# Rotary halves by transfer, an even filling row in layer 2, 136-column pooling bands and an early Exp table in a two-layer transformer kernel

## The chip, the cores and the metric

The kernel runs on one core of one Trainium2 chip. The time is the device time of one execution in microseconds. The kernel before takes 1686.69 us (median of 3 runs, 1686.47 to 1686.74). Five engines work side by side, each through its own list of instructions in order: PE (matmuls), ACT (activations, casts, copies), DVE (elementwise work and reductions), POOL (a little elementwise work) and SP, which only issues transfers (DMAs). The order on each engine is fixed when the program is built; an instruction waits on semaphores for the engines or transfers that it depends on.

## What is computed

Two transformer layers on 256 tokens of width 1024, with 256 context tokens beside them. A layer is a half feed-forward step, a mixing step and a second half feed-forward step; the last layer updates only the tokens, not the context. In the mixing step one projection gives queries, keys and values for a windowed attention of 4 heads, an input `u` for average pooling over 4 groups of 64 channels, and queries, keys and values for a grouped attention (8 query heads, 2 key heads). The queries and keys of the grouped attention are normalised per head and rotated by position:

```
def _rope_axis(x, ang):
    m = x.shape[-1] // 2
    x1, x2 = x32[..., :m], x32[..., m:]
    return jnp.concatenate([x1 * cos - x2 * sin, x1 * sin + x2 * cos], axis=-1)
...
out = jnp.concatenate([_rope_axis(x[..., :half], ang_row), _rope_axis(x[..., half:], ang_col)], axis=-1)
...
y = (mean - u32.reshape(bn, n, POOL_GROUPS, POOL_GC))     # mean over windows of 2, 4, 8, 16 tokens
y = jnp.einsum('blgc,gcd->blgd', y, w_pool)
```

So within a head of 64 channels, channel i of the first 16 is paired with i + 16, and channel i of the next 16 after 32 with i + 16 again. In between, pieces of the modulation weights `w_ada` for the next phase are multiplied with the two condition vectors.

## The kernel before, in words

Matrices are held feature-major (128 features on the partitions, tokens along the free axis). A float32 product is made of three PE matmuls of split operands (L351, L352, L353, called mm3 below): each weight piece of 1 MB or 0.5 MB is loaded by SP into a `raw` buffer, cast by ACT (L309) and its remainder formed by DVE (L312, "split of a weight"); after the split the `raw` buffer is free and SP may issue the next load into it.

The mixing step in program order: keys and values (`evac_k` writes the grouped keys `kc` with the gain; `k_post` at L915 makes their norms and rotates them), windowed queries, windowed values, and then `run` (L1094), a loop over attention jobs. A job is two heads and 128 tokens: `scores` (L1012, L1013: four matmuls into two PSUM banks), DVE's maximum (L1028 adds the bias of the windowed heads, L1029 reduces), ACT's Exp (L1037), DVE's division by the sum (L1042). Two jobs later `flip` (L1056: eight transposes by PE, L1064: copies by ACT) and, when a pair of heads is whole, `pv` (L1086). Layer 1 has 18 jobs (six of them for the context), layer 2 has 12: four windowed (j0 to j3) and eight grouped ones (j4 to j11).

PE would wait for the softmax between jobs, so other work is put there. `fill(us)` calls `piece()` until a planner's clock has advanced by `us`; `piece()` takes, in this order, the rest of the in-projection (`rest_in`: four chunks c0 to c3 of the grouped queries, 24 matmuls each, then `u`, 24 matmuls for 128 tokens), `pv` of finished windowed heads, `pooled` (L1178), and then by turns a piece of the out-projection and a quantum of the `w_ada` products (L181). How much goes between two jobs is the row `FILL[l]`: entries 2n and 2n+1 stand after the scores of job n and before the flip of job n-2 (for the first two jobs only entry 2n is used, as nothing is flipped yet). The clock has no relation to the chip: matmuls and pooling add fixed numbers to it by `tick`, and `later(us, f)` puts `f` into the program when the clock has moved on by `us`. So a change of a `tick`, of a `FILL` entry or of a `later` moves instructions on all engines.

A finished chunk is evacuated by ACT twice: `qc` with the gain (L1148) and its square (L1150); `qstat` (L1155, weights `hind`) sums the squares per head on PE. After each pair of chunks `q_post` rotates the pair and makes the reciprocal norms on DVE (twelve small instructions, L392 to L1130). Before a grouped job is scored its queries are split by ACT (L892) and DVE (L893). `before(n)` makes the grouped keys at job 2 (ACT L881, DVE L884).

`rotate` (L900): PE multiplies `q` with a 128x128 matrix `rot` of +1 and -1 (L903) that exchanges and signs the halves, DVE multiplies the result with the sine (L906), POOL multiplies `q` with the cosine in place (L907), and DVE adds (L910). It is called once for the keys and twice for the queries in each layer, five matmuls of 256 columns per layer.

`pooled` (L1178) multiplies `u` with band matrices: for each of the 4 groups two matmuls of 128 columns (L1185, bands `pmd`) and two of 8 columns (L1186, L1187, `edge`) for the tokens across the border between the two blocks. It is called twice in layer 1 (tokens, context) and once in layer 2. ACT copies the result `y` (L1190), PE multiplies it with `pwbd` (L1195).

PSUM has 5 banks for products and scores, 2 for transposes and statistics (`aux`), and 1 for the `w_ada` products.

Of the kernel before, what the change touches and what calls it, by code (L numbers as in the profile page):

```python
# [38 lines left out]
FILL = ((3.3, 2.6, 1.8, 2.6, 3.3, 5.5, 0, 0.6, 3.3, 0, 0.6, 1.2, 1.8, 0.6, 4.2, 2.6, 2.6, 0, 0, 0.6, 4.2, 0.6, 1.2, 0, 2.6, 1.2, 0, 1.8, 2.6, 1.2, 2.6, 0, 0.6, 1.2, 0.6, 0.6, 0, 0, 5.5, 2.6), (3.3, 0.6, 2.6, 3.3, 0.6, 3.3, 5.5, 0, 1.8, 1.8, 0.6, 1.8, 0.6, 5.5, 0, 1.2, 1.2, 1.2, 1.2, 1.2, 4.2, 1.2, 0.6, 0.6, 1.8, 0, 2.6, 0.6))  # L39
# [11 lines left out]
def dit_kernel(  # L51
# [790 lines left out]
    def attention(l, a, both):  # L842
# [55 lines left out]
        def rotate(q, n):  # L898

            rp = aux_bank()  # L900
            rv = rp[:, 0:n * TX].rearrange("p (c t) -> p c t", c=n)
            for i in range(n):
                PE.matmul(out=rv[:, i, :], lhsT=rot, rhs=q[:, i, :], start=True, stop=True)  # L903
# [2 lines left out]
            DVE.tensor_tensor(out=tv, in0=rv, in1=rope[:, 1:2, :].to_broadcast([128, n, TX]), op=ALU.mult)  # L906
            POOL.tensor_tensor(out=q, in0=q, in1=rope[:, 0:1, :].to_broadcast([128, n, TX]), op=ALU.mult)  # L907
# [27 lines left out]
        def evac_k(v, pss):  # L935
            lo, hi = v * TX, v * TX + TX
            ACT.activation(out=ksq[:, lo:hi], in_=pss[1][:, 0:TX], func=AF.Square)
            ACT.activation(out=kc[:, lo:hi], in_=pss[1][:, 0:TX], func=AF.Copy, scale=kng(l))
            ACT.copy(out=vcT[:, lo:hi], in_=pss[1][:, TX:NT])

            def split():
                for hp in range(2):
# [180 lines left out]
        def q_post(j):  # L1123

            rotate(qc[:, 2 * j:2 * j + 2, 0:TX], 2)

            def norm():
                o = slice(j * nb * 4, (j + 1) * nb * 4)
                rq = rsqrt(qst[0][:, o], nb * 4, 1.0 / 64)
                DVE.tensor_scalar(out=rq8[:, o], in0=rq, scalar1=0.125, scalar2=None, op0=ALU.mult)  # L1130
                turned[j] = True
            later(2.0, norm)

        def rest_in():

            qst.append(mm_bank())
            for j in range(2):
# [39 lines left out]
        def pooled(v):  # L1177
            ps = mm_bank()  # L1178
            pv_ = ps.rearrange("p (c t) -> p c t", c=2)
            for g in range(4):  # L1180
# [3 lines left out]
                for tb in range(2):  # L1184
                    PE.matmul(out=o[:, tb * 128:(tb + 1) * 128], lhsT=ug[tb], rhs=pmd[tb][:, g * 128:(g + 1) * 128], start=(g < 2 and tb == 0), stop=False)  # L1185
# [362 lines left out]

def _constants():

    ident = np.eye(128, dtype=np.float32)
    rot = np.zeros((128, 128), np.float32)
    for f in range(128):
        i = f % 32
        if i < 16:
            rot[f + 16, f] = -1.0
        else:
            rot[f - 16, f] = 1.0
# [47 lines left out]
```

## Time and profile before

| | |
|---|---|
| median of 3 runs | 1686.69 us (1686.47 to 1686.74) |
| profiled execution | 1686.64 us |
| its span, first to last instruction | 1684.9 us |
| mean granted PE clock | 0.998 |
| busy share PE, DVE, ACT, POOL | 99%, 63%, 39%, 3% |
| instructions | 23252 |
| transfers | 246.97 MB, 147 GB/s |
| attention of layer 1, of layer 2 | about 453 to 560 us, 1389 to 1472 us |

Times in the views are microseconds from the start of the span. A row of the timeline has start, duration, engine, line, operation, written tile and read tiles, and in square brackets the idle time before it and what ended that. Several like instructions in a row are merged ("x8"); one program matmul of float32 operands that are not split appears as two records. A row of the waits has the waiting engine and line, the releasing engine, tile and line, the total, the count and the longest.

### The profile page before, as it was taken

Reading aid. Unit: us, or ns where it says so; the run is one execution under the profiler, and the core shown is the slowest. Engines: PE = TensorE matmul, PEld = TensorE weight load, DVE = VectorE, ACT = ScalarE, POOL = GpSimd, SP = SyncE. Lnnn points to the kernel's source line nnn. Section 1 sums busy time; section 2 is a strip of 40 time slices with the busy share of each in tenths; the row PEclk is TensorE's granted clock in tenths of the full one; section 3 lists DMA queues with packets and bytes.
Section 4 is the critical chain, followed back from the end, with each engine's and each line's share of the span. In section 5 each row is a group of like instructions: output and inputs, shape, how many; then the busy total and the mean of one; then the engine's idle time right before and its main releaser. Section 6 shows DMA issues by size and latency. Waiting matters only on the chain. (4 is left out here: it accounts for less than half of the span.)

```text
span 1684.9 us, 23252 instructions
## 1 busy us (share of the span) xinstructions
PE 1660.0 (99%) x9256; PEld 1401.6 (83%) x9256; DVE 1055.3 (63%) x1850; ACT 663.8 (39%) x1119; POOL 47.8 (3%) x67
## 2 busy tenths in 40 slices
PE   8999999999999999999999999999999999999997
PEld 5788888889896798888888898888888897799996
DVE  5676567667666776666764476545533567785665
ACT  4332323324556643223233243213232255664543
POOL 0000200000010000000000000020000000010000
PEclk9999999999999999999999999999999999999999
DMA  9755546531305425554553325564533223566551
GB/s 332 206 190 171 161 153 194 167 120 58 113 26 176 132 67 173 166 163 138 175 156 120 87 79 178 161 170 159 155 112 95 81 76 137 202 195 193 179 174 74
DMA packets 284932, 246.97 MB, mean 147 GB/s; under 512 B 9345, under 2 KB 249098, under 8 KB 282776
## 3 DMA queue, kind: packets, MB, share of 16 engines
q1 hardware_dynamic: 281992, 241.30, 46.2%
q0 software_dynamic: 1088, 2.15, 0.6%
q10 hardware_dynamic: 1744, 2.04, 0.4%
q8 instruction: 73, 1.20, 0.3%
q14 instruction: 35, 0.29, 0.1%
HBM read 244.40 MB, written 2.00 MB: 146 GB/s over the span
## 5 line engine op out<-in xcount | busy, mean ns | idle before, releaser
L351 PE MATMUL mm<-act,w 128*128 128x512 f32 (+1 forms) x2016 | 739.1, 367 | 0.0
L352 PE MATMUL mm<-act,w 128*128 128x512 f32 (+1 forms) x2016 | 733.0, 364 | 0.3 <-DVE act L435 0.3
L353 PE MATMUL mm<-act,w 128*128 128x512 f32 (+1 forms) x2016 | 732.9, 364 | 0.0
L312 DVE TENSOR_TENSOR w<-raw,w 128x1024 fp32r<-128x1024 f32 (+1 forms) x307 | 367.6, 1206 | 222.3 <-ACT w L309 221.9
L351 PEld LDWEIGHTS mm<-act,w 128*128 128x128 f32 x2016 | 380.5, 189 | 75.2 <-issue 14.1
L353 PEld LDWEIGHTS mm<-act,w 128*128 128x128 f32 x2016 | 380.4, 189 | 59.7
L352 PEld LDWEIGHTS mm<-act,w 128*128 128x128 f32 x2016 | 380.7, 189 | 59.1 <-DVE act L435 0.5
L309 ACT CAST w<-raw 128x1024 fp32r<-128x1024 f32 (+1 forms) x308 | 313.3, 1031 | 118.8 <-PE mm L353 96.9
L224 DVE SCALAR_TENSOR_TENSOR ada_acc<-ada_raw,sc,ada_acc 128x512 f32<-128x512 f32 x308 | 215.9, 747 | 37.9 <-DMA ada_raw<-in_w_ada_dram 20.9
L562 ACT CAST act<-gf 128x512 fp32r<-128x512 f32 x66 | 40.9, 620 | 269.9 <-DVE gf L559 269.9
L556 ACT ACTIVATE sil<-mm 128x512 f32<-128x512 f32 x66 | 39.3, 596 | 189.4 <-PE mm L353 184.5
L465 DVE SCALAR_TENSOR_TENSOR hT<-mm,hgt,hT 128x256 f32<-128x256 f32 x144 | 63.5, 480 | 76.9 <-PE mm L353 76.6
L559 DVE TENSOR_TENSOR gf<-sil,mm 128x512 f32<-128x512 f32 x65 | 44.7, 687 | 89.5 <-PE mm L353 75.7
L644 PE MATMUL mm<-act,w 128*128 128x258 f32 x352 | 100.2, 285 | 0.0
L645 PE MATMUL mm<-act,w 128*128 128x258 f32 x352 | 99.6, 283 | 0.0
L646 PE MATMUL mm<-act,w 128*128 128x258 f32 x352 | 99.5, 283 | 0.0
L563 DVE TENSOR_TENSOR act<-gf,act 128x512 fp32r<-128x512 f32 x66 | 45.7, 693 | 45.3 <-ACT act L562 45.3
L645 PEld LDWEIGHTS mm<-act,w 128*128 128x128 f32 x352 | 66.8, 190 | 0.3 <-DVE act L618 0.2
L644 PEld LDWEIGHTS mm<-act,w 128*128 128x128 f32 x352 | 66.6, 189 | 0.1
L646 PEld LDWEIGHTS mm<-act,w 128*128 128x128 f32 x352 | 66.4, 189 | 0.0
L377 ACT ACTIVATE sq<-hT 128x256 f32<-128x256 f32 (+1 forms) x45 | 22.5, 500 | 90.8 <-DVE hT L465 90.8
L441 ACT ACTIVATE act<-nt,modT 128x256 fp32r<-128x256 f32 x80 | 39.8, 508 | 37.8 <-DVE nt L440 37.8
(198 smaller groups left out, 1412.1 us busy)
## 6 DMA issues: line engine op xcount, KB each, us to landing
raw<-in_ffn_up_dram SPq DMA_DIRECT2D x170, 512.0 KB
ada_raw<-in_w_ada_dram SPq DMA_DIRECT2D x192, 256.0 KB
raw<-in_ffn_down_dram SPq DMA_DIRECT2D x35, 1024.0 KB
raw<-in_w_ada_dram SPq DMA_DIRECT2D x16, 1024.0 KB
raw<-in_w_in_dram SPq DMA_DIRECT2D x10, 1024.0 KB
raw<-in_ffn_down_dram SPq DMA_DIRECT2D x12, 768.0 KB
raw<-in_w_out_dram SPq DMA_DIRECT2D x8, 1024.0 KB
raw<-in_w_ada_dram SPq DMA_DIRECT2D x12, 512.0 KB
```

The source lines that it names most:

```text
L224: DVE.scalar_tensor_tensor(out=o, in0=raw, scalar=col, in1=o, op0=ALU.mult, op1=ALU.add)
L309: ACT.copy(out=wh, in_=sl)
L312: eng.tensor_tensor(out=wl, in0=sl, in1=wh.bitcast(F32), op=ALU.subtract)
L351: PE.matmul(out=ps, lhsT=wh, rhs=ah, start=start and i == 0, stop=False)
L352: PE.matmul(out=ps, lhsT=wh, rhs=al, start=False, stop=False)
L353: PE.matmul(out=ps, lhsT=wl, rhs=ah, start=False, stop=stop and i == last)
L465: DVE.scalar_tensor_tensor(out=hT[:, k, cols], in0=ps, scalar=gate[:, k, v:v + 1], in1=hT[:, k, cols], op0=ALU.mult, op1=ALU.add)
L559: DVE.tensor_tensor(out=u[:, 0:n], in0=s[:, 0:n], in1=pb[:, 0:n], op=ALU.mult)
L563: DVE.tensor_tensor(out=gl, in0=uv, in1=gh.bitcast(F32), op=ALU.subtract)
L644: PE.matmul(out=ps[:, 0:NX], lhsT=wh, rhs=ah, start=k == 0, stop=False)
L645: PE.matmul(out=ps[:, 0:NX], lhsT=wh, rhs=al, start=False, stop=False)
L646: PE.matmul(out=ps[:, 0:NX], lhsT=wl, rhs=ah, start=False, stop=k == KD - 1)
```

## The change

1. **Rotation.** The matrix `rot` and its matmuls are gone. `swapped` copies the four blocks of 32 partitions crosswise with four SP transfers into `ks` or `qs`: for the keys right after `kc` of the tokens is written, for the queries after each pair of chunks is evacuated. For this the 64 channels of a head are permuted on the host (`HEAD_ORDER`, in the columns of `w_in` for grouped queries and keys and in their gains), so that partners lie 32 partitions apart; the signs go into the sine table. DVE multiplies the swapped tile with the sine in place, both operands now in SBUF, and adds; POOL's cosine product is as before, but writes `q` in place after the transfers have read it. `q_post` is put 5.5 after its pair of chunks by the clock, before 3.0. The tiles `bands`, `qs` and `ks` lie in a part of the layer's activation tile that was unused.
2. **Layer 2's row of FILL**: 28 entries of 1.7 (sum 47.6) in place of 28 different ones (sum 48.9). Layer 1's row is the same.
3. **Pooling**: two matmuls of 136 columns for each group, the second one accumulating on the columns 120 to 256; `tick` 1.1 in place of 1.7.
4. **Exp table**: before the first scores of a layer ACT runs a dummy Exp on one column, so that the table is loaded there.

```diff
-FILL = ((3.3, 2.6, ...), (3.3, 0.6, 2.6, 3.3, 0.6, 3.3, 5.5, 0, 1.8, 1.8, 0.6, 1.8, 0.6, 5.5, 0, 1.2, 1.2, 1.2, 1.2, 1.2, 4.2, 1.2, 0.6, 0.6, 1.8, 0, 2.6, 0.6))
+FILL = ((3.3, 2.6, ...), (1.7,) * 28)
...
+        bands = carve(1088, "p (b g t) -> p b g t", b=2, g=4)
+        qs = carve(1024, "p (c t) -> p c t", c=4)
+        ks = carve(256, "p (c t) -> p c t", c=1)
...
-        def rotate(q, n):
-            rp = aux_bank()
-            rv = rp[:, 0:n * TX].rearrange("p (c t) -> p c t", c=n)
-            for i in range(n):
-                PE.matmul(out=rv[:, i, :], lhsT=rot, rhs=q[:, i, :], start=True, stop=True)
-            t = tmp.tile([128, 512], F32, tag="t2k", bufs=T2K, name="rot_t")
-            tv = t[:, 0:n * TX].rearrange("p (c t) -> p c t", c=n)
-            DVE.tensor_tensor(out=tv, in0=rv, in1=rope[:, 1:2, :].to_broadcast([128, n, TX]), op=ALU.mult)
+        def swapped(dst, src):
+            for p0 in range(0, 128, 32):
+                SP.dma_start(out=dst[p0 ^ 32:(p0 ^ 32) + 32], in_=src[p0:p0 + 32])
+        def rotate(q, other, n):
             POOL.tensor_tensor(out=q, in0=q, in1=rope[:, 0:1, :].to_broadcast([128, n, TX]), op=ALU.mult)
-            def add():
-                DVE.tensor_tensor(out=q, in0=q, in1=tv, op=ALU.add)
-            later(1.5, add)
+            DVE.tensor_tensor(out=other, in0=other, in1=rope[:, 1:2, :].to_broadcast([128, n, TX]), op=ALU.mult)
+            later(1.5, lambda: DVE.tensor_tensor(out=q, in0=q, in1=other, op=ALU.add))
...
             if v:
                 later(0.1, split)
             else:
+                swapped(ks[:, 0], kc[:, 0:TX])
                 split()
...
-            ACT.dma_start(out=pmd[b].rearrange("p (g t) -> p g t", g=4), in_=k_pool[b])
+            ACT.dma_start(out=bands[:, b], in_=k_pool[b])
...
+            if not PT and not sums:
+                warm = small.tile([128, 8], F32, tag="nm", bufs=6, name="nm")
+                ACT.activation(out=warm[:, 0:1], in_=ones, func=AF.Exp)
...
-                later(3.0, lambda j=j: q_post(j))
+                swapped(qs[:, 2 * j:2 * j + 2], qc[:, 2 * j:2 * j + 2, 0:TX])
+                later(5.5, lambda j=j: q_post(j))
...
-                for tb in range(2):
-                    PE.matmul(out=o[:, tb * 128:(tb + 1) * 128], lhsT=ug[tb], rhs=pmd[tb][:, g * 128:(g + 1) * 128], start=(g < 2 and tb == 0), stop=False)
-                PE.matmul(out=o[:, 128:136], lhsT=ug[0], rhs=edge[:, 0, g, :], start=False, stop=False)
-                PE.matmul(out=o[:, 120:128], lhsT=ug[1], rhs=edge[:, 1, g, :], start=False, stop=(g >= 2))
-            tick(1.7)
+                PE.matmul(out=o[:, 0:136], lhsT=ug[0], rhs=bands[:, 0, g], start=g < 2, stop=False, skip_group_check=True)
+                PE.matmul(out=o[:, 120:256], lhsT=ug[1], rhs=bands[:, 1, g], start=False, stop=g >= 2, skip_group_check=True)
+            tick(1.1)
```

In the rows of order below, a line number is that of the kernel which the rows are from: in the kernel after, most lines stand one or two lines earlier (Exp is L1036 there, the chunk's evacuation L1147 and L1149, the transposes L1055). On ACT at the start of layer 2's attention, before, Exp of job j0 (two heads), the evacuation of chunk c0 (`qkv` and `qsq`), Exp of j1, then c1, then the four casts of the grouped keys (`K`), then Exp of j2:

```order
L982 DMA pmd<-in_k_pool_dram 128x512 x2
L1037 ACT_TABLE_LOAD
L1037 ACTIVATE P,sums<-mm,nm 128x512 x2
L1148 ACTIVATE qkv<-mm,colsB 128x256
L1150 ACTIVATE qsq<-mm 128x256
L1037 ACTIVATE P,sums<-mm,nm 128x512 x2
L1148 ACTIVATE qkv<-mm,colsB 128x256
L1150 ACTIVATE qsq<-mm 128x256
L881 CAST K<-qkv 64x512 x4
L1037 ACTIVATE P,sums<-mm,nm 128x512 x2
```

Now, on the same engine at the same place, the table is loaded first, and the Exp of both j0 and j1 stand before the first chunk:

```order
L977 DMA qkv<-in_k_pool_dram 128x544 x2
L1005 ACT_TABLE_LOAD
L1005 ACTIVATE nm<-ones 128x1
L1036 ACTIVATE P,sums<-mm,nm 128x512 x4
L1147 ACTIVATE qkv<-mm,colsB 128x256
L1149 ACTIVATE qsq<-mm 128x256
L880 CAST K<-qkv 64x512 x4
L1036 ACTIVATE P,sums<-mm,nm 128x512 x2
L1147 ACTIVATE qkv<-mm,colsB 128x256
```

The evacuation of c0 moved behind the Exp of j1, and that of c1 behind the casts of the keys and the Exp of j2. On PE the number of in-projection matmuls between the scores of j0 and j1 goes from 36 to 18, between j1 and j2 from 30 to 18.

On PE at the end of layer 2's attention, before (the out-projection's matmuls that lie between are left out at the marks): the scores of the last job j11, a `w_ada` quantum, the transposes of j9, a quantum, those of j10 and of j11, the transposes of the modulation (`adasb`), and the last `pv`:

```order
L1012 MATMUL mm<-K,qst 128x512
L1013 MATMUL mm<-K,qst 128x512
...
L181 MATMUL ada<-raw,sc 32x512 x4
L1056 MATMUL aux<-ident,P 128x128 x8
...
L181 MATMUL ada<-raw,sc 32x512 x4
...
L1056 MATMUL aux<-ident,P 128x128 x8
...
L1056 MATMUL aux<-ident,P 128x128 x8
L249 MATMUL aux<-ident,adasb 128x128 x4
L1086 MATMUL mm<-PT,qkv 64x256 x16
```

Now, on PE at the same place, from the transposes of the modulation on (only the second half of j11's scores is left out):

```order
L247 MATMUL aux<-ident,adasb 128x128 x4
L1055 MATMUL aux<-ident,P 128x128 x4
L1085 MATMUL mm<-PT,qkv 64x256 x16
L1055 MATMUL aux<-ident,P 128x128 x4
L1011 MATMUL mm<-K,qst 128x512
L1012 MATMUL mm<-K,qst 128x512
...
L1055 MATMUL aux<-ident,P 128x128 x24
L1085 MATMUL mm<-PT,qkv 64x256 x16
```

All other pieces stand before the last scores, and 24 transposes in a row follow them. On SP in layer 2, before, the loads of the in-projection, the first out-projection piece and the `w_ada` pieces:

```order
L152 DMA raw<-in_w_in_dram 128x8x256 x4
L150 DMA raw<-in_w_in_dram 128x8x128 x4
L152 DMA raw<-in_w_in_dram 128x8x256
L152 DMA raw<-in_w_out_dram 128x4x512
L157 DMA raw<-in_w_ada_dram 128x2048 x4
```

Now, on SP at the same place, with the swaps of the keys (`32x256`) and of the two query pairs (`32x2x256`) among them:

```order
L150 DMA raw<-in_w_in_dram 128x8x256 x4
L148 DMA raw<-in_w_in_dram 128x8x128 x2
L900 DMA qkv<-qkv 32x256 x4
L148 DMA raw<-in_w_in_dram 128x8x128 x2
L150 DMA raw<-in_w_in_dram 128x8x256
L150 DMA raw<-in_w_out_dram 128x4x512
L155 DMA raw<-in_w_ada_dram 128x2048
L900 DMA qkv<-qkv 32x2x256 x4
L155 DMA raw<-in_w_ada_dram 128x2048
L900 DMA qkv<-qkv 32x2x256 x4
L155 DMA raw<-in_w_ada_dram 128x2048 x2
```

The first query swap stands behind one load of `w_ada`, the second behind two; before, the four loads of `w_ada` followed each other. The other loads keep their order.

More of the change, by code (lines that the diff above doesn't have):

```diff
@@ L38 @@
 DEPTH = (2, 2)
[L39 removed]
+FILL = ((3.3, 2.6, 1.8, 2.6, 3.3, 5.5, 0, 0.6, 3.3, 0, 0.6, 1.2, 1.8, 0.6, 4.2, 2.6, 2.6, 0, 0, 0.6, 4.2, 0.6, 1.2, 0, 2.6, 1.2, 0, 1.8, 2.6, 1.2, 2.6, 0, 0.6, 1.2, 0.6, 0.6, 0, 0, 5.5, 2.6), (1.7,) * 28)
 PACE = (0.8, 0.8, 0.8, 0.8, 0.7, 0.8)
@@ L56, in dit_kernel @@
     na_rpb, pool_w, pool_scale, q_norm_g, k_norm_g, final_g,
-    k_ident, k_rot, k_rope, k_mask, k_pool, k_edge,
+    k_ident, k_rope, k_mask, k_pool,
     out,
@@ L807, in attn_prep @@
             ACT.dma_start(out=mask, in_=k_mask)
-            ACT.dma_start(out=rot, in_=k_rot)
-            ACT.dma_start(out=edge, in_=k_edge)
             ACT.dma_start(out=rope, in_=k_rope.rearrange("s p t -> p s t"))
@@ L977, in attention @@
             pass
-        pmd = [tmp.tile([128, 512], F32, tag="t2k", bufs=T2K, name="pmd") for _ in range(2)]
         for b in range(2):
-            ACT.dma_start(out=pmd[b].rearrange("p (g t) -> p g t", g=4), in_=k_pool[b])
+            ACT.dma_start(out=bands[:, b], in_=k_pool[b])
         rq8 = small.tile([128, 40], F32, tag="rq8", bufs=1, name="rq8")
@@ L1546, in dit_kernel, with _laid_out @@
         flush()
+HEAD_ORDER = np.r_[0:16, 32:48, 16:32, 48:64]
+def _laid_out(name, a):
+    a = np.array(a)
+    if name == "w_in":
+        cols = a[:, :, 1024:1664]
+        a[:, :, 1024:1664] = cols.reshape(a.shape[0], a.shape[1], 10, 64)[..., HEAD_ORDER].reshape(cols.shape)
+    elif name in ("q_norm_g", "k_norm_g"):
+        a = a[:, HEAD_ORDER]
+    return a
 def _constants():
     ident = np.eye(128, dtype=np.float32)
[L1552 to L1558, printed above, removed]
     pos = np.arange(256)
@@ L1563, in _constants @@
     head = np.concatenate([ar, ar, ac, ac], axis=1)
-    ang = np.concatenate([head, head], axis=1).T
-    rope = np.stack([np.cos(ang), np.sin(ang)]).astype(np.float32)
+    ang = np.concatenate([head[:, HEAD_ORDER]] * 2, axis=1).T
+    sign = np.where(np.arange(128) % 64 < 32, -1.0, 1.0)[:, None]
+    rope = np.stack([np.cos(ang), np.sin(ang) * sign]).astype(np.float32)
     col = np.arange(128) % 64
@@ L1575, in _constants @@
             pool[t, g, t] -= np.float32(1.0)
-    blocks = np.stack([pool[0:128, :, 0:128], pool[128:256, :, 128:256]])
-    edge = np.stack([pool[0:128, :, 128:136], pool[128:256, :, 120:128]], axis=1)
-    return {"k_ident": ident, "k_rot": rot, "k_rope": rope, "k_mask": mask, "k_pool": np.ascontiguousarray(blocks), "k_edge": np.ascontiguousarray(edge)}
+    bands = np.stack([pool[0:128, :, 0:136], pool[128:256, :, 120:256]])
+    return {"k_ident": ident, "k_rope": rope, "k_mask": mask, "k_pool": np.ascontiguousarray(bands)}
 _INS = ['x', 'c', 'ctx', 'c_ctx', 'w_ada', 'b_ada', 'norm_g', 'ffn1_up', 'ffn1_down', 'ffn2_up', 'ffn2_down',
         'w_in', 'w_out', 'na_rpb', 'pool_w', 'pool_scale', 'q_norm_g', 'k_norm_g', 'final_g']
-_CONST = ['k_ident', 'k_rot', 'k_rope', 'k_mask', 'k_pool', 'k_edge']
+_CONST = ['k_ident', 'k_rope', 'k_mask', 'k_pool']
 _OUTS = [((1, 256, 1024), 'float32')]
@@ L1594 @@
     for name in _INS + _CONST:
-        a = np.ascontiguousarray(inputs[name] if name in inputs else consts[name])
+        a = np.ascontiguousarray(_laid_out(name, inputs[name]) if name in inputs else consts[name])
         arrays[f"in_{name}_dram"] = a
```

6 lines of the change are left out of this document (2 added, 4 removed).

## The prediction

> **What bounds the kernel now.** I read the page's shares first, then the list of what PE waits for, then stretches of 10 and 20 us around the two attention phases, and last the timelines of the places that the change touches. The page's row of shares:
>
> ```profile
> PE 1660.0 (99%) x9256; PEld 1401.6 (83%) x9256; DVE 1055.3 (63%) x1850; ACT 663.8 (39%) x1119; POOL 47.8 (3%) x67
> ```
>
> PE is busy for 1660.0 of 1684.9 us of span; the others have room. So a gain must take PE work away or close one of PE's few gaps, and a loss must open gaps. PE's waits over the whole program (waiting line, releaser, total, count, longest):
>
> ```profile
> PE aux L927 <- DVE rs_y L401: 2.0, 2, 1.3
> PE mm L1012 <- ACT P L1037: 1.3, 1, 1.3
> PE aux L1056 <- ACT PT L1064: 1.1, 1, 1.1
> PE ada L181 <- DMA raw<-in_w_ada_dram: 1.0, 1, 1.0
> ...
> PE mm L1155 <- DVE rs_v L392: 0.4, 1, 0.4
> ...
> PE aux L249 <- ACT PT L1064: 0.2, 1, 0.2
> PE mm L1185 <- issue: 0.2, 1, 0.2
> ```
>
> Apart from L927, all of these lie in layer 2's attention and sum to 4.2. A stretch of layer 1's attention and two of layer 2's (window, length, busy PE, PEld, DVE, ACT, POOL, clock, DMA share, GB/s):
>
> ```profile
> 500.00:520.00 20.00, 20.00 (x184) 15.53 (x185) 12.35 (x33) 13.80 (x32) 0.00 (x0) 1.00 0.21 62
> ...
> 1400.00:1410.00 10.00, 9.62 (x74) 9.16 (x73) 8.10 (x25) 6.08 (x13) 1.30 (x1) 1.00 0.01 2
> 1410.00:1420.00 10.00, 9.83 (x89) 9.24 (x88) 8.97 (x27) 6.04 (x13) 1.30 (x1) 1.00 0.32 107
> ```
>
> Layer 1 has PE full while DVE and ACT have 6 to 8 of 20 us free: PE work taken away there is time won. In layer 2 DVE is busy for 8 to 9 of 10 us and PE has gaps already: there the order decides.
>
> **Rotation, on PE.** The pair of query matmuls before, the next two products, the three elementwise groups, and the keys' wait (timeline and groups):
>
> ```profile
> 1411.08 1.11 PE L903 MATMUL aux<-qkv,rot 128*128 128x256 f32 x4
> 1411.84 0.47 PE L351 MATMUL mm<-w,act 128*128 128x256 f32 x1
> 1412.15 0.28 PE L352 MATMUL mm<-w,act 128*128 128x256 f32 x1
> 1412.27 0.29 PE L353 MATMUL mm<-w,act 128*128 128x256 f32 x1
> ...
> L906 DVE TENSOR_TENSOR rot_t<-aux,rope x6: 417/688/693, 439.5 to 1412.2; 128x512 f32<-128x512 f32 x4, 128x256 f32<-128x256 f32 x2
> ...
> L907 POOL TENSOR_TENSOR qkv<-qkv,rope x6: 1297/1302/1808, 431.1 to 1412.3; 128x512 f32<-128x512 f32 x4, 128x256 f32<-128x256 f32 x2
> ...
> 1380.83 0.88 PE L927 MATMUL aux<-ident,rs_y 128*64 128x128 f32 x12 [0.76 <-DVE rs_y L401]
> ```
>
> From L903's start to L351's are 0.76, and the first product after it starts 0.19 later than the 0.12 from L352 to L353; part of that stays after any switch. I take 0.8 for a query pair, 1.6 a layer. The keys' matmuls save nothing: L927 waits for DVE's norms, which do not depend on them, so that wait grows by what is saved. DVE's two products per rotation stay at 0.69 each if two SBUF operands cost what one of PSUM did, and POOL's stays at 1.30.
>
> **The swaps.** No transfer between SBUF tiles is in the trace. The nearest row is POOL's 64 KB transfer:
>
> ```profile
> braw<-tab POOLq DMA_DIRECT2D x32, 64.0 KB, 2.4
> ```
>
> A query swap has four of that size; with some 0.3 each for SP's issues it lands about 1.3 + 2.4 = 3.7 after its chunk. The keys' swap has ten us and more before it is used: hidden. The first query swap of layer 1 lands about as late as L906 starts now, with POOL's 1.30 behind it, so the sum on DVE comes up to 1 us later; PE has no gap near it, so it costs 0 to 1, and I take 0.5. The second ones stand on SP behind a `w_ada` load, but DVE wants them some 8 us later.
>
> **Pooling.** The 16 matmuls of a call before, first and following instruction:
>
> ```profile
> 508.40 0.60 PE L1185 MATMUL mm<-pmd,qkv 128*64 128x128 f32 x4
> ...
> 510.60 0.66 PE L1061 MATMUL aux<-ident,P 128*128 128x128 f32 x4
> ```
>
> 2.2 from one start to the other, or 2.0 without the 0.2 of a switch. The columns stay the same, 128 + 128 + 8 + 8 or 136 + 136 a group; the matmuls are halved. So the gain lies between 0 (columns alone) and 1.0 a call (number alone). I take the price per column of the rotation's matmuls, 0.76 for 512 columns: 0.20 for 136, 1.6 a call, 0.4 saved; 0.8 in layer 1 and 0.4 in layer 2. Layer 1 then gives -1.6 - 0.8 + 0.5 = -1.9. The loads of the bands keep their place on ACT's queue.
>
> **Layer 2: the row of FILL and the table.** ACT, DVE and PE at its start, before:
>
> ```profile
> 1388.82 0.40 PE L1012 MATMUL mm<-K,qst 128*128 128x512 f32 x1
> 1396.00 0.50 PE L1012 MATMUL mm<-K,qst 128*128 128x512 f32 x1 [1.32 <-ACT P L1037]
> ...
> 1393.88 1.28 ACT L1037 ACT_TABLE_LOAD   x1 [2.59 <-DVE nm L1029]
> 1395.17 0.69 ACT L1037 ACTIVATE P<-mm,nm 128x512 f32<-128x512 f32 x1
> 1396.51 0.47 ACT L1148 ACTIVATE qkv<-mm,colsB 128x256 f32<-128x256 f32 x1
> 1399.39 2.52 ACT L881 CAST K<-qkv 64x512 fp32r<-64x512 f32 x4
> ...
> 1392.65 0.43 DVE L1028 TENSOR_TENSOR mm<-mm,bm 128x256 f32<-128x256 f32 x1
> 1393.11 0.69 DVE L1029 TENSOR_REDUCE nm<-mm 128x1 f32<-128x512 f32 x1
> 1393.72 0.42 DVE L1028 TENSOR_TENSOR mm<-mm,bm 128x256 f32<-128x256 f32 x1
> ...
> 1401.93 0.69 DVE L884 TENSOR_TENSOR K<-qkv,K 64x512 fp32r<-64x512 f32 x1 [1.22 <-ACT K L881]
> ```
>
> I walk the new order through these durations, in before's clock: scores of a job 1.0, mm3 0.36, DVE 1.07 per windowed head (1392.65 to 1393.72), Exp 0.88 with the reading of its sum (0.69 and the 0.19 quoted under *End*), a chunk's evacuation 0.75 (0.47 and a shorter square, overlapped).
> The table goes into ACT's idle 2.59, so Exp of j0 starts at 1393.8, not 1395.17. By the Trainium skill ("ScalarE: Activation LUTs", section "What ACT_TABLE_LOAD costs") a switch is a load of about 1283 ns and a drain of about 1380 ns, 2.66 us; by it the early table would be worth twice as much. The trace has the 1.28 and Exp right behind it, with no drain.
> *First bank.* PE has j0 at 1388.8, 18 matmuls, j1 to 1392.9, the last six of c0 to 1393.6. Four banks hold scores and one c0; c1 needs one more, free when Exp of j0's first head has read it, 1394.6: **1.0**. j2's second bank 0.2.
> *Chunks' squares.* Exp of j0 and j1 run at DVE's pace to 1397.9 and c0 is evacuated by 1398.6; its `hind` comes at 1398.2: 0.4. Then the casts of the keys to 1401.2, DVE's remainders to 1401.8, j2's maxima to 1404.0, its Exp to 1404.9, c1 evacuated by 1405.6; PE is at c1's `hind` by 1402.9: **2.7**.
> *Queries of j4.* These rows price the chain and, the last two, what follows it:
>
> ```profile
> 1407.38 0.16 DVE L392 TENSOR_SCALAR rs_v<-mm 128x8 f32<-128x8 f32 x1
> ...
> 1409.58 0.17 DVE L1130 TENSOR_SCALAR rq<-rs_y 128x8 f32<-128x8 f32 x1
> 1410.95 0.85 DVE L893 TENSOR_TENSOR qst<-qkv,qst 64x256 fp32r<-64x256 f32 x2
> ...
> 1405.58 0.49 DVE L1042 TENSOR_SCALAR P<-P,sums 128x512 f32<-128x512 f32 x1
> ...
> 1419.37 2.36 DVE L312 TENSOR_TENSOR w<-raw,w 128x1024 fp32r<-128x1024 f32 x2
> 1426.93 1.06 PE L181 MATMUL ada<-raw,sc 128*32 128x512 f32 x8 [0.99 <-DMA raw<-in_w_ada_dram]
> ```
>
> After: c1 is written at 1405.3, the swap lands at 1409. PE scores j3 by 1407.2; DVE finishes its maxima at 1409.3 and two divisions (0.6 each with the reciprocal) at 1410.5, then the sine product, the split of a weight that stands between it and the sum (1.2, half of the row's 2.36), the sum: 1413.1; the norms, 1407.38 to 1409.66, 2.28: 1415.4; half of L893: 1415.9. PE is ready for j4 at 1413.2: **2.7**. Queued behind PE's wait are c3's `hind`, `u` and everything else.
> *Behind j4.* The two splits (1419.37) that free the buffers for `w_ada` follow the later rotation, so the third quantum, which waits 0.99 now, waits about 1.0 (0.7 to 1.7), `pwbd` waits for `y`, copied by ACT behind Exp of j5, 1.2 (0.7 to 2.0), an out-projection product 0.3, a later quantum 0.6 (0 to 1.1).
> *End.* The last job before:
>
> ```profile
> 1458.23 0.47 PE L1012 MATMUL mm<-K,qst 128*128 128x512 f32 x1
> 1461.43 0.19 ACT L1037 ACTIVATION_READ_ACCUMULATOR P<-mm,nm,rq 128x1 f32 x1
> 1465.39 1.09 ACT L1064 COPY PT<-aux 128x512 f32<-128x512 f32 x2
> ```
>
> Its Exp ends 3.4 after its scores begin. Before, 9 us of PE work lay behind the scores; after, only the 24 transposes (2.6). Two banks take the transposes, and the six copies stand on ACT behind that Exp, 0.54 each: the fifth ends 6.1 after the scores' start, when the last `pv` can begin; PE is through its transposes at 3.6: **2.5**.
>
> Together 1.0 + 0.2 + 0.4 + 2.7 + 2.7 + 1.0 + 1.2 + 0.3 + 0.6 + 2.5 = 12.6 of waits in place of 4.2: +8.4; less 1.6 and 0.4 of PE work: +6.4 in layer 2. With layer 1's -1.9 the sum is +4.5 on the profiled 1686.64: 1691.1. The profiled execution lies 0.05 under the median, so nothing is added. With the waits' bounds taken as 9.5 and 15 and pooling's as above this case reaches from 1687 to 1694.
>
> **Rivals.** 0.2% is 3.4 us, about what a measurement of this kernel can tell from no change.
> *The waits are one chain (within 0.2%).* c1's `hind` and j4 both wait for the same DVE and ACT work; if DVE, which has slack from 1397 to 1402, is earlier by a few instructions than I walked, one of the two 2.7 is absorbed, and the sum is +1.8, 1688.4. For it: DVE's idle 1.22 ahead of L884. Against: the casts that end it have their fixed place behind c0.
> *Only the forced waits stay (faster).* The bank (1.0) and the end (2.5) follow from the order alone. If the even row, which has work after every job, hides the rest as layer 1's hides all of its own, waits are 3.5 in place of 4.2, and with 2.0 of PE work and layer 1's 1.9 the sum is -4.6: 1682.0. It decides if c1's evacuation ends before 1403 in before's clock, and Q of j4 before 1413. For it: layer 1's full windows; against it: DVE's 8.10 and 8.97 of 10 us.
> *The swap is slow (still slower).* If four transfers between partitions take what a `w_ada` load takes, about 5 us (its buffer is free when the splits end at 1421.73, and PE waits for it until 1426.93), each swap is 2.5 later; j4 and the second pair wait that much more in part, layer 1's first pair opens a gap of 1: +3.5 on the forecast, 1694.6. By the Trainium skill ("DMA: Bandwidth & Descriptors", section "Queues, rings and completion order") a queue's transfers on one engine start in order, so a swap issued behind a 1 MB load waits for that; no trace here shows a swap.
>
> **How the numbers follow.** The walk is fixed by the order and by durations from rows, but ten small waits have to be right, and errors on one engine are partly absorbed by the next. I give the forecast 0.37, the slow swap 0.08, one chain 0.30, only forced waits 0.25. The likeliest is 1691.1, slower. The range leaves out some 0.12 below 1681.5 and 0.06 above 1694.5. Faster 0.25, same 0.30, slower 0.45.
>
> **What would show it.** In the profile after: layer 1's attention shorter by about 2 with PE full; L927's waits longer by 0.3 to 0.4; L1154 waiting for ACT's `qsq` by 2 to 3; L1011 of j4 waiting for `qst`; the last L1085 waiting for `PT` by 2 to 3; in all some 13 us of PE waits between 1388 and 1475. If L1154 and j4 show under 1 each, the walk is wrong in its main part; if layer 1 has gaps, the swap is.

## The result and the profile after

The kernel after takes 1695.75 us (median of 4 runs, 1693.93 to 1696.31), the kernel before beside it 1686.58 (4 runs, 1686.07 to 1686.74). The ratio is 1.0052, interval 1.0039 to 1.0066: slower by 9.2 us. The forecast was 1691.1, so its direction came true and its size did not: the time lies beyond the upper end of the range, 1694.5. The profiled execution took 1695.37 with a span of 1693.6 and a mean granted clock of 0.996 (before: 0.998), 8.73 over before's.

The shares of the engines after:

```profile
PE 1658.0 (98%) x9188; PEld 1398.3 (83%) x9188; DVE 1054.9 (62%) x1850; ACT 664.4 (39%) x1121; POOL 46.7 (3%) x67
```

PE has 68 matmul records fewer, but only 2.0 us less busy time, and its span has grown by 8.7. Where it waits within layer 2's attention, 1380 to 1490 (waiting line, releaser, total, count, longest):

```profile
PE mm L1154 <- ACT qsq L1149: 2.5, 1, 2.5
PE ada L179 <- DMA raw<-in_w_ada_dram: 2.3, 2, 1.8
PE aux L1055 <- ACT PT L1063: 2.1, 2, 1.9
PE mm L1011 <- DVE qst L892: 2.0, 1, 2.0
PE mm L349 <- ACT P L1036: 1.0, 1, 1.0
PE mm L349 <- ACT w L307: 0.9, 1, 0.9
PE mm L351 <- DVE w L310: 0.8, 1, 0.8
PE aux L247 <- ACT PT L1063: 0.7, 1, 0.7
PE mm L1193 <- ACT y L1188: 0.6, 1, 0.6
```

These are 12.9 us of waits in place of 4.2. Stretches of layer 1's and of layer 2's attention, and then the six microseconds behind each of the four longest waits (the columns are those of the prediction's windows; the clock is the third figure from the end):

```profile
500.00:520.00 20.00, 20.00 (x164) 14.02 (x163) 15.13 (x42) 13.24 (x30) 0.32 (x1) 1.00 0.32 107
1400.00:1410.00 10.00, 8.63 (x57) 8.25 (x58) 7.36 (x16) 6.26 (x15) 1.29 (x1) 0.83 0.11 26
1410.00:1420.00 10.00, 7.95 (x38) 7.33 (x36) 7.46 (x23) 3.47 (x8) 1.28 (x1) 0.66 0.42 134
...
1401.50:1407.50 6.00, 6.00 (x36) 5.62 (x37) 3.94 (x9) 4.02 (x9) 1.29 (x1) 0.72 0.18 44
1412.70:1418.70 6.00, 6.00 (x24) 5.61 (x25) 4.71 (x11) 1.70 (x4) 1.28 (x1) 0.50 0.28 94
1430.40:1436.40 6.00, 5.35 (x35) 2.76 (x33) 3.33 (x10) 4.03 (x9) 0.00 (x0) 1.00 1.02 403
1474.90:1480.90 6.00, 5.81 (x48) 4.47 (x48) 0.76 (x3) 2.50 (x5) 0.00 (x0) 1.00 0.01 3
```

Layer 1 is as full as before. In layer 2 the granted clock falls, where before it was 1.00: to a mean of 0.72 behind the first wait of the list and to 0.50 behind the wait of j4, while PE is busy all the time (6.00 of 6.00). The timeline of PE shows what that does to a matmul (start, duration; brackets hold the idle time before):

```profile
1401.37 0.61 PE L1154 MATMUL mm<-hind,qsq 128*128 128x2 f32 x4 [2.50 <-ACT qsq L1149]
...
1404.18 0.42 PE L350 MATMUL mm<-act,w 128*128 128x256 f32 x1
1404.39 0.41 PE L351 MATMUL mm<-act,w 128*128 128x256 f32 x1
...
1406.89 0.28 PE L351 MATMUL mm<-act,w 128*128 128x256 f32 x1
1407.00 0.28 PE L349 MATMUL mm<-act,w 128*128 128x256 f32 x1
...
1412.61 0.79 PE L1011 MATMUL mm<-K,qst 128*128 128x512 f32 x1 [2.05 <-DVE qst L892]
```

At 1404 two products follow each other in 0.21, at 1407 in 0.11: the same instruction takes about twice as long for some microseconds behind a wait.

Where the 8.7 came from shows when like instructions of PE in the two traces are set side by side (after less before): +0.5 at 160 us, -0.1 at 454, -2.3 at 511, -3.4 from 791 to 1335, -4.1 at 1389, and +8.7 from 1572 to the end. So all the work ahead of layer 2's attention became 4.1 faster, and that attention 12.8 slower. Within that attention the new row moves instructions against each other, so that shifts of single ones measure nothing there.

### The profile page after: what moved, and what is told of

The parts are those of the page before. It is cut to its first block, busy times and chain, and to the rows that moved or that the text cites. A ratio compares the mean times of both kernels' runs of the same rounds, so it can differ in the third digit from the quotient of the medians.

```text
span 1693.6 us, 23162 instructions
## 1 busy us (share of the span) xinstructions
PE 1658.0 (98%) x9188; PEld 1398.3 (83%) x9188; DVE 1054.9 (62%) x1850; ACT 664.4 (39%) x1121; POOL 46.7 (3%) x67
## 4 chain that ended last, share of the span: by engine, by line
PE 89%; DVE 5%; ACT 2%; DMA 2%; issue 1%; SPq 0%; POOL 0%; ACTq 0%; DVEq 0%; POOLq 0%
PE mm L349 24%; PE mm L350 24%; PE mm L351 23%; PE mm L643 3%; PE mm L642 3%; PE mm L644 2%; PE mm L1474 1%; PE mm L1085 1%; DVE w L310 1%; DVE nm L1028 1%; DMA raw<-in_w_ada_dram 1%; PE aux L1055 1%; DMA xin<-in_ffn_up_dram 1%; PE ada L230 1%; PE aux L351 1%
```

## The experiments

**The row of FILL by itself.** Two kernels exchange only layer 2's row: in the first the kernel after gets the old one, in the second the kernel before gets the even one.

```diff
-FILL = ((3.3, 2.6, ...), (1.7,) * 28)
+FILL = ((3.3, 2.6, ...), (3.3, 0.6, 2.6, 3.3, 0.6, 3.3, 5.5, 0, 1.8, 1.8, 0.6, 1.8, 0.6, 5.5, 0, 1.2, 1.2, 1.2, 1.2, 1.2, 4.2, 1.2, 0.6, 0.6, 1.8, 0, 2.6, 0.6))
```

> The changed kernel with layer 2's old row of FILL; rotation, pooling and table stay changed. Theory 1 (the even row makes the whole loss: its waits of 12.9 us on PE in layer 2, and the slowed clock behind two of them): the waits fall back to about 4, the granted clock stays at 1.00 between 1380 and 1480, and the time is that of the kernel before less what the changed profile shows already ahead of layer 2's attention (4.1 us), less 1.6 for layer 2's query rotation and 1.0 for its pooling, and up to 1.3 for the table: 1678.5 to 1681. Theory 2 (the swaps make the loss, since j4's queries come late behind them): the wait ahead of j4 stays near 2 us with slow clock behind it, and the time is above 1684.

Measured: 1680.83 us (7 runs, 1680.44 to 1683.37), ratio 0.9972 (0.9961 to 0.9983). Its longer waits in layer 2, and the six microseconds behind the longest:

```profile
PE aux L1055 <- ACT PT L1063: 2.3, 1, 2.3
PE mm L1184 <- ACT qkv L970: 1.8, 1, 1.8
PE ada L179 <- DMA raw<-in_w_ada_dram: 1.7, 1, 1.7
```

```profile
1428.90:1434.90 6.00, 6.00 (x32) 3.71 (x33) 2.83 (x10) 3.83 (x10) 0.00 (x0) 0.72 0.01 3
```

The even row costs 14.9 us (1695.75 less 1680.83), more than the whole loss; without it the change is a gain of 5.5. Here, too, in the profiled execution (1683.37, the longest of the seven), a wait of 2.3 is followed by a clock of 0.72, which had been expected to stay at 1.00. The wait ahead of j4 is gone, although the swaps are those of the kernel after.

The second, the even row on the kernel before:

```diff
-FILL = (..., (3.3, 0.6, 2.6, 3.3, 0.6, 3.3, 5.5, 0, ...))
+FILL = (..., (1.7,) * 28)
```

> The kernel before with only layer 2's row of FILL made even; the rotation stays on PE. Theory 1 (the row): waits of some 10 to 13 us in place of 4.2 and a stretch of slowed clock behind the longest of them: 1695 to 1700. Theory 2 (the swaps): the queries come sooner from PE's rotation than from the swaps, the wait ahead of j4 is under 1, no slowed clock: 1687 to 1691.

Measured: 1698.52 us (5 runs, 1697.26 to 1702.03), ratio 1.0078 (1.0064 to 1.0092), 12.2 over before. It has waits of 2.32 (ended 1395.7), 2.36 (1411.9), 2.13 (1456.7) and 2.77 (1475.9); the windows behind them:

```profile
1395.80:1401.80 6.00, 6.00 (x35) 5.63 (x36) 3.72 (x9) 4.78 (x12) 0.00 (x0) 0.72 0.00 0
1412.00:1418.00 6.00, 4.53 (x37) 4.29 (x38) 3.46 (x14) 2.51 (x6) 0.00 (x0) 1.00 0.30 89
1456.80:1462.80 6.00, 6.00 (x46) 4.01 (x43) 2.91 (x9) 3.05 (x7) 0.00 (x0) 1.00 1.01 383
1476.00:1482.00 6.00, 6.00 (x41) 5.47 (x43) 0.74 (x3) 2.66 (x5) 0.00 (x0) 0.74 0.18 44
```

The row is slow on the old rotation as well, so it is not the swaps that make it so. Two of its four waits over 2 us are followed by a lower clock, two are not.

**The three other parts, one at a time on the kernel before.** The edit of each is that part of the diff shown above; in the pooling's kernel `tick` stays at 1.7. First the rotation with its swaps and the later `q_post`:

> The kernel before with the rotation by transfers alone (with its step at 5.5 of the clock); PE's order is that of before without the ten rotation matmuls. By the prediction's terms: 1.6 us a layer for the query pairs, nothing for the keys, 0.5 lost in layer 1: -2.7, 1683.6. By the changed profile, where the keys' waits already came sooner by 0.5 in each layer: -3.5 to -4.2, 1682 to 1683. Rival (the swaps come late in layer 2's denser stretch and j4 waits): a wait on the queries of 1 us or more, and 1684 or above.

Measured: 1683.61 us (11 runs, 1682.68 to 1686.58), ratio 0.9987 (0.9978 to 0.9996), -2.7. It has one new wait, at the old pooling, and this window behind it:

```profile
PE mm L1183 <- ACT w L308: 2.8, 1, 2.8
```

```profile
1414.60:1420.60 6.00, 6.00 (x62) 4.40 (x63) 5.62 (x17) 2.00 (x4) 0.00 (x0) 1.00 0.38 124
```

A wait of 2.8 with no fall of the clock in this execution. The runs of this kernel spread over 3.9 us, with mean granted clocks from 0.996 to 0.999.

The pooling bands alone:

> The kernel before with the pooling of two matmuls of 136 columns a group alone, its step of the clock left at 1.7 so that no other instruction moves. If columns set the price: no change. By the prediction's term (0.20 for 136 columns): -1.2, 1685.1. If the number of matmuls sets it, half of 2.0 to 2.2 a call: -3.0 to -3.3 over three calls, less up to 1 that a later wait of layer 2 takes back: 1683 to 1684.

Measured: 1683.80 us (11 runs, 1683.43 to 1684.34), ratio 0.9986 (0.9977 to 0.9995), -2.55. A call and the instruction behind it:

```profile
508.29 0.45 PE L1182 MATMUL mm<-qkv 128*64 128x136 f32 x4
...
509.37 1.09 PE L1059 MATMUL aux<-ident,P 128*128 128x128 f32 x8
```

From one start to the other are 1.08, where before they were 2.2. Half as many matmuls over the same columns took half as long: an 8-column matmul had cost about as much as a 128-column one.

The early table alone, ahead of the first scores:

```diff
+            if not PT and not sums:
+                warm = small.tile([128, 8], F32, tag="nm", bufs=6, name="nm")
+                ACT.activation(out=warm[:, 0:1], in_=ones, func=AF.Exp)
```

> The kernel before with the dummy Exp ahead of each layer's first scores alone. If the first Exp of layer 2 comes 1.28 sooner, PE's wait of 1.3 for a bank there goes down to about 0 and the time falls by up to 1.3, less what the next wait (0.4, for a reciprocal norm) takes back: -0.5 to -1.3. If DVE's maxima set the end of that chain anyway: no change.

Measured: 1685.50 us (11 runs, 1685.05 to 1685.83), ratio 0.9995 (0.9986 to 1.0004): -0.85, within what the interval leaves open. In its trace the 1.3 us for which PE waited for the first Exp are gone, and PE's wait for the sums of squares is 0.5.

The three parts sum to -6.1, and the kernel with all three and the old row gave -5.5: they nearly add up.

**Are the waits of c1 and of j4 one chain?** The keys' casts move from job 2 to job 3 in layer 2, so that c1's evacuation no longer stands behind them.

```diff
-KEYS_AT = (2, 2)
+KEYS_AT = (2, 3)
```

> The changed kernel with the grouped keys of layer 2 made at job 3 in place of job 2, so that ACT evacuates c1 before its four casts of the keys and not behind them. Theory A (the two long waits are separate): the wait of 2.5 us for c1's square goes with the slow clock behind it, the wait ahead of j4 stays at 2, the time falls by 3.5 to 4.5 us. Theory B (both hang on one chain of DVE and ACT): the first wait goes, but j4 waits 3 to 5 us in place of 2.05, since DVE's maxima of j3 now stand behind the keys' remainders; the time falls by 1 to 2.5 us.

Measured: 1692.94 us (5 runs, 1692.49 to 1693.16), ratio 1.0039 (1.0027 to 1.0052), 2.8 less than the kernel after. The wait of j4's scores, and the window behind it:

```profile
PE mm L1011 <- DVE qst L892: 5.0, 1, 5.0
```

```profile
1410.30:1416.30 6.00, 6.00 (x24) 5.62 (x25) 3.66 (x11) 1.70 (x4) 1.48 (x1) 0.50 0.01 3
```

c1's wait is gone, and j4's grew from 2.05 to 5.0: as a sum 4.55 became 5.0. PE only waits at another place for the same chain on ACT and DVE. The time fell by a little more than the 1 to 2.5 that the expectation gave to one chain. j4 is scored at 1410.24 instead of 1412.61, 2.4 earlier. On DVE ahead of it the maxima of j3 start 0.8 earlier (1402.64 for 1403.42), the division behind them takes 0.48 instead of 1.14, and the split of a weight, 1.22 in the kernel after, no longer stands between the sine product and the sum.

**Does PE's idle time cost more than itself?** The kernel after gets eleven more matmuls of 256 columns whose results nobody reads, at the two places where PE waited longest: six ahead of c1's sums of squares, five ahead of the first scores of j4.

```diff
+        def busy(n):
+            for _ in range(n):
+                PE.matmul(out=qst[0][:, 256:512], lhsT=ident, rhs=rope[:, 0, :], start=True, stop=True)
...
+                        if l == 1 and cchunk == 1:
+                            busy(6)
...
+            if l == 1 and kind == "gqa" and hs[0] == 0 and t == 0:
+                busy(5)
```

> The changed kernel with eleven matmuls of 256 columns more that compute nothing that is used: six ahead of the sums of c1's squares, five ahead of j4's scores, about the length of the two gaps of 2.50 and 2.05 us there (0.38 each). Theory 1 (the slowed clock is set off by PE's idle time and costs time by itself): the granted clock stays at 1.00 there, and although PE has 4 us more to do, the time falls by 3 to 5 us, to 1691 to 1693. Rival (the slow clock costs nothing since the other engines set the pace there, or it is not set off by idle time): the time stays at 1695 to 1697, and the extra work shows as longer by what does not fit into the gaps.

Measured: 1693.49 us (5 runs, 1691.48 to 1693.87), ratio 1.0039 (1.0027 to 1.0052), 2.3 less than the kernel after, with more work, but less than the 3 to 5 expected. The two stretches in the profiled execution:

```profile
1400.00:1410.00 10.00, 9.05 (x68) 8.22 (x67) 7.64 (x18) 7.28 (x17) 1.31 (x1) 1.00 0.20 42
1410.00:1420.00 10.00, 9.76 (x71) 8.03 (x70) 7.24 (x20) 3.78 (x7) 1.47 (x1) 1.00 0.34 118
```

The clock is 1.00 in both, where after it was 0.83 and 0.66. Nothing was taken from the chain that PE waits for; only the idle time was filled. The profiled execution is the fastest of the five (1691.48, mean clock 0.998); the others have mean clocks of 0.996 and 0.997, so they still lost some clock, at places that no trace shows.

Then the reverse: a wait put into layer 1 of the kernel before, where PE had none. One matmul, also with a result that nobody reads, reads c0's square right behind the instruction of ACT that writes it, so that PE has to wait for ACT; in a second kernel POOL first multiplies that square by one.

```diff
+                    if l == 0 and cchunk == 0:
+                        PE.matmul(out=qst[0][:, 256:512], lhsT=ident, rhs=sq[:, 0:256], start=True, stop=True)
```

> The kernel before with one matmul of 256 columns more in layer 1's attention, where PE has no gap: it reads the square of chunk c0 right behind c0's last product and so makes PE wait for ACT, some 1.3 to 2 us; its result isn't used. If idle time costs its length alone: the time rises by the gap and 0.4 for the matmul. The same by the rule that slow clock follows only gaps of about 2 us and more: clock 1.00 behind it.

Measured: 1691.27 us (7 runs, 1689.55 to 1691.53), ratio 1.0027 (1.0016 to 1.0038), +5.15. The wait was 2.82, longer than expected; the window behind it:

```profile
463.00 0.70 PE L1154 MATMUL mm<-qsq,ident 128*128 128x256 f32 x2 [2.82 <-ACT qsq L1150]
```

```profile
463.10:469.10 6.00, 6.00 (x22) 4.82 (x22) 3.96 (x8) 3.31 (x7) 0.00 (x0) 0.72 0.00 0
```

Of the 5.15 the wait makes 2.82 and the matmul about 0.4; 1.9 are left. The window lost 0.28 of 6.0, 1.7. Two of the runs took 1689.6 and 1689.7, with a mean granted clock of 0.998 instead of 0.997: about 1.7 less than the others.

```diff
+                        POOL.tensor_tensor(out=sq, in0=sq, in1=ones.to_broadcast([128, 512]), op=ALU.mult)
```

> The same with one product on POOL in between (the square times one, 128x512), so that PE waits some 1.3 us longer, about 2.7 to 3.5. If a longer gap sets off the slow clock: 1.5 to 3.5 us more than the longer gap alone makes, with a stretch of granted clock below 0.9 behind it in the profile and a wider spread between runs. If idle time costs its length alone: 1.3 to 1.5 us above the short gap and clock 1.00.

Measured: 1692.58 us (5 runs, 1692.47 to 1693.29), ratio 1.0039 (1.0025 to 1.0053), +6.46, with

```profile
464.73 0.70 PE L1154 MATMUL mm<-qsq,ident 128*128 128x256 f32 x2 [3.94 <-POOL qsq L1153]
```

```profile
464.80:470.80 6.00, 6.00 (x22) 4.83 (x22) 3.37 (x8) 1.94 (x5) 0.97 (x2) 0.72 0.00 0
```

3.94 and 0.4 leave 2.1. So the wait of 3.9 cost no more beyond itself than the one of 2.8.

**Which half of the row?** The kernel after with the old first ten entries and even ones of 1.4 behind:

```diff
-FILL = (..., (1.7,) * 28)
+FILL = (..., (3.3, 0.6, 2.6, 3.3, 0.6, 3.3, 5.5, 0, 1.8, 1.8) + (1.4,) * 18)
```

> The changed kernel with the first ten entries of layer 2's old row (jobs j0 to j4) and 1.4 for the other 18, about the same sum. The old row in full gave 1680.8, the even one 1695.75. By the changed profile the start of the row carries the bank's wait, the two long waits and the slow clock behind them, the end the 2.5 us behind the last transposes: so about 3 of the 15 us should stay: 1683 to 1686. Rival (the even end is as costly as the even start, since the loads and transposes wait there as well): 1688 or above.

Measured: 1687.08 us (11 runs, 1684.5 to 1688.37), ratio 1.0003 (0.9994 to 1.0012). That is 6.2 over the kernel with the old row, a miss at the upper side: if the parts add up, the later entries make 6.2 of the row's 14.9 and the first ten 8.7 (the later ones were 1.4 here and 1.7 in the even row). PE waits twice for the copies of the transposes, 4.4 in all, once at the very end (2.11, ended 1465.9, clock 0.72 behind it).

**A better version.** With the old row the swaps' kernel still waits 1.8 for the copy of `u` at the pooling. Five altered entries put the pooling later:

```diff
-(3.3, 0.6, 2.6, 3.3, 0.6, 3.3, 5.5, 0, 1.8, 1.8, 0.6, 1.8, 0.6, 5.5, ...)
+(3.3, 0.6, 2.6, 3.3, 0.6, 3.3, 3.5, 0, 2.6, 1.0, 1.8, 2.0, 0.6, 5.5, ...)
```

> The changed kernel with layer 2's old row of FILL (as in the first experiment) and five entries of it altered (5.5, 0, 1.8, 1.8, 0.6, 1.8 become 3.5, 0, 2.6, 1.0, 1.8, 2.0), so that the transposes of j1 and the scores of j4 stand ahead of the pooling instead of behind it. In the first experiment PE waits 1.8 for the copy of u, 1.7 for a load and 2.3 for transposes' copies, with slow clock behind. If these waits come from the pooling standing too close behind u: the first goes, the others shrink, 1677 to 1679.5. If the loads set the pace there, the load's wait grows by what is saved: 1680 to 1681.

Measured: 1683.80 us (11 runs, 1683.44 to 1684.17), ratio 0.9985 (0.9976 to 0.9994): 3.0 slower than with the old row, a miss.

```profile
PE mm L1185 <- ACT qkv L970: 4.6, 1, 4.6
```

The copy of `u`'s last part is put into the program only when `rest_in` is called again, so later work for PE put it behind the Exp of j4 on ACT. In the next kernel the copy is written directly behind the last matmul:

```diff
-                    if k % 4 == 3:
+                    if k == 3:
                         yield
                 (ACT.copy if tb % 2 else DVE.tensor_copy)(out=dst[:, tb, :], in_=ps[:, 0:TX])
+                yield
```

> The kernel of the experiment with the pooling behind j4, and besides the copy of a piece of u put into the program right behind its last matmul, not when its generator is called again. There the pooling waits 4.6 for that copy, since it is recorded only when the next piece is asked for, behind j4's Exp on ACT. If that is the cause: the 4.6 goes, the loads' wait of 1.4 grows to 2 or 3, no slow clock: 1678 to 1680.5, below the first experiment's 1680.8. If the pooling is late for another reason (the loads, j4's maxima): 1682 or above.

Measured: 1679.50 us (5 runs, 1679.31 to 1680.46), ratio 0.9962 (0.9949 to 0.9976), 6.8 less than before. This is the fastest kernel here. One wait over 0.2 us is left in its layer 2's attention, and it is followed by a clock of 0.72 once more, where 1.00 and a wait for the loads had been expected:

```profile
PE mm L1194 <- ACT y L1189: 2.6, 1, 2.6
```

```profile
1420.20:1426.20 6.00, 6.00 (x31) 2.64 (x32) 4.96 (x14) 3.99 (x11) 0.00 (x0) 0.72 0.88 326
```

## Why the prediction was right in direction and wrong in size

**Layer 2's walk** was right, in its sum (12.9 of waits for 12.6) and mostly in its parts: the first bank 1.0 for 1.0, c1's `hind` 2.50 for 2.7, the queries of j4 2.05 for 2.7, `pwbd` 0.6 for 1.2, the last transposes 1.9 (behind them the `pv`, which had been expected to wait) for 2.5. The loads of `w_ada` make 2.3 for 1.0 and 0.6. c0's 0.4 did not come; two products of the out-projection wait 0.9 and 0.8 for 0.3, and the transposes of the modulation wait 0.7, which the walk did not have. So about 2.6 of the forecast terms did not come and about as much came at other places: that the sum fits to 0.3 is in part luck. On ACT the reason of c1's wait stands as it was walked, the table, the casts of the keys, and the square that ends the wait:

```profile
1387.24 1.28 ACT L1005 ACT_TABLE_LOAD   x1
...
1394.32 2.52 ACT L880 CAST K<-qkv 64x512 fp32r<-64x512 f32 x4
...
1400.94 0.38 ACT L1149 ACTIVATE qsq<-mm 128x256 f32<-128x256 f32 x1
```

**The step that failed** is the next one, "12.6 of waits in place of 4.2: +8.4; less 1.6 and 0.4 of PE work: +6.4". It took PE's work behind each wait at the durations of before. It was not in the sum that PE comes out of a long wait at half of its clock. The ten-microsecond rows of the kernel after give 0.17 x 10.0 = 1.7 behind c1's wait and 0.34 x 10.0 = 3.4 behind j4's, whose slow stretch reaches beyond the six microseconds shown: together 5.1. With that the account of layer 2 is 8.7 of waits, less 1.6 for the rotation and 1.1 for the pooling, and 5.1 for the clock: 11.1 of the 12.8 that the traces show. About 1.7 are not placed. The miss was larger than the two times show: layer 2's attention became 12.8 slower for a forecast of 6.4, and the work ahead of it 4.1 faster for a forecast of 1.9, by the keys and the pooling. That the lower clock follows from the idle time, and not from the row or the swaps, was shown from both sides: filled waits had 1.00, and a wait made in layer 1 of the kernel before brought 0.72.

**Rotation.** PE's 1.6 a layer less the 0.5 of the late sum were 1.1; the traces show about 1.0 in layer 1. For the keys the forecast was nothing, since L927 would wait longer for DVE's norms. They gave 0.6 in each layer, and the wait did not grow: 0.54 in layer 2 (now L922), before 0.76.

```profile
1376.75 1.09 PE L922 MATMUL aux<-ident,rs_y 128*64 128x128 f32 x16 [0.54 <-DVE rs_y L399]
```

What made the norms earlier was not tried. The part by itself gave -2.7, with one new wait of 2.8 in it and two old waits gone, so that it equals the forecast's terms (-1.6 twice and +0.5) by luck.

**Pooling** was mis-sized: 0.4 a call forecast, 1.1 measured, the upper end of the bounds. The price per column came from matmuls of 256 columns, and for short ones the number counts.

**The table** gave 0.85 by itself. In the whole change its share can't be read off, as the new row moves the same instructions: the casts of the keys, at 1394.32 for 1399.39, stand 5.1 earlier, 1.0 more than the scores of j0.

**The rivals.** "The swap is slow" has not come true in time: layer 1 has no new wait except 0.3, though the swaps landed later than estimated (last section). "Only the forced waits stay" is excluded by the list of waits. Of "the waits are one chain" the mechanism is right, as the kernel with the later keys shows, but not its consequence: both parts of the chain were there in full length, 4.55 together, because DVE was not earlier than walked. The condition that it named, DVE being earlier by a few instructions, was not met.

## What to carry to other kernels

When a reordering makes new waits on an engine that is otherwise full, don't price a wait by its length alone: here a wait of PE of more than 2 us mostly cost 1.7 us more by the clock behind it, at times 3.4, while the clock stayed full behind waits of 1.95 and less; so, going by these traces, waits that are spread out should cost less than a long one of the same sum. A row that spreads work evenly by a planner's clock is not even for the engines: look on each helping engine at what its fixed-place work now stands in front of. Test the parts of a mixed change apart; here three parts gained 6 us, and one row of numbers hid them.

## What the runs showed of the hardware

**The clock behind a wait.** In the profiled executions of the kernels here lie 27 waits of PE between 1.4 and 5.0 us within the two attention phases. Behind the 12 of 1.95 and less the clock was 1.00 each time. Behind the 15 of 2.05 and more it was below 0.8 in 12, at 0.72 to 0.74 (mean over the six microseconds) in 9, 0.60 in one, 0.50 in two; in three (2.13, 2.36, 2.78) it stayed at 1.00. 0.72 is what 3.4 us at half clock make of six. So the length of a wait alone does not decide.

The record of the clock in these traces shows what does. In all 14 of them every change of the clock lies a whole number of steps of 3.413 us behind the first moment at full clock. With the traces cut into these steps, PE was idle for 1.93 us or more in 12 steps at full clock, and each of the 12 was followed by half clock; the most idle step that was not followed by it had 1.83. Here are the step of c1's wait, the one behind it and the step of j4's wait in the kernel after, and then the two steps on which the wait of 2.78 in the rotation's kernel falls:

```profile
1398.95:1402.37 3.42, 1.00 (x9) 1.00 (x10) 1.94 (x6) 3.14 (x9) 0.00 (x0) 1.00 0.00 0
1402.37:1405.78 3.41, 3.41 (x14) 3.03 (x14) 2.26 (x6) 1.45 (x5) 0.47 (x1) 0.50 0.31 77
1409.19:1412.61 3.42, 1.37 (x14) 1.14 (x12) 2.98 (x16) 1.77 (x4) 0.00 (x0) 1.00 0.71 216
...
1410.04:1413.45 3.41, 1.67 (x14) 1.47 (x13) 3.27 (x8) 2.22 (x6) 0.94 (x1) 1.00 0.29 84
1413.45:1416.87 3.42, 2.38 (x33) 2.39 (x34) 3.42 (x5) 1.55 (x3) 0.32 (x1) 1.00 0.01 2
```

The 2.78 leave 1.74 of idle time in one step and 1.04 in the next, and the clock stays. The waits of 2.13 and 2.36 are divided as well, with at most 1.50 and 1.27 of idle time in a step. Of the 3.94 of the long wait in layer 1, 2.31 fall into one step and 1.63 into another, and one step at half clock follows, as behind the 2.82, which fits that it cost no more beyond its length. A step at half clock loses half of 3.413, 1.7. If a wait falls differently on the steps in each execution, the same wait costs 1.7 or nothing; that would explain the two runs of the 2.82 that were about 1.7 less. The rule was read from the finished traces, and no kernel was built to test it; why two steps at half clock follow j4's wait, though PE is busy all through the first of them, is open.

The Trainium skill ("TensorE: Matmul & The Clock Gate", section "What's actually happening") has PE at half clock after an idle window of about 3.4 us, and full clock after about as long a busy one, with a window that runs freely. The length of the steps and the way they run on through the whole program agree with that. That 1.93 us of idle time in a step are enough does not agree with a wholly idle window as the condition.

**Swaps and POOL.** The first query swap of layer 2, POOL's product behind it, and three of DVE's divisions (start, duration):

```profile
1401.07 2.59 SPq L900 DMA_DIRECT2D qkv<-qkv  x4
...
1405.31 1.29 POOL L904 TENSOR_TENSOR qkv<-qkv,rope 128x512 f32<-128x512 f32 x1 [15.10 <-DMA qkv<-qkv]
...
1405.74 1.14 DVE L1041 TENSOR_SCALAR P<-P,sums 128x512 f32<-128x512 f32 x1
1406.99 0.49 DVE L1041 TENSOR_SCALAR P<-P,sums 128x512 f32<-128x512 f32 x1
...
1415.71 1.53 DVE L1041 TENSOR_SCALAR P<-P,sums 128x512 f32<-128x512 f32 x1
```

SP takes 2.59 to issue four transfers, 0.65 each where 0.3 was estimated; all four have landed 4.2 after the first issue, for 3.7. And a division takes 0.49 by itself, but 1.14 and 1.53 beside POOL's product (1405.31 to 1406.60, and another from 1415.68 to 1416.96). The prediction let them run side by side at no cost. The Trainium skill ("GPSIMD Engine Reference", section "Specifications") has POOL and VectorE share their SBUF interfaces, with contention for some of VectorE's instructions; these rows agree. The second swap was issued 0.44 behind a `w_ada` load (1409.24 and 1409.68), and POOL's product behind it starts 6.0 after its first issue, at 1415.68: 1.8 later than behind the first. The load ahead of it is the likely reason; no run tried it.
